# A hybrid decoder layer on one core: eight weight column groups in the opening instead of seven

## The chip, the core and the metric

The kernel runs on one core of one Trainium2 chip. Times are device microseconds of one whole execution. The kernel before took 734.72 us (median of three runs, 734.35 to 735.94). The profiled execution, from which all rows in this document come, took 734.0 us, of which 732.2 us are the profiled span.

The core's engines are called PE (TensorE), DVE (VectorE), ACT (ScalarE), POOL (GpSimd) and SP (SyncE, which only issues transfers here). Each runs its own list of instructions in order and waits on the others through semaphores. PE writes its results to eight banks of 128 x 512 float32 values (PSUM); ACT and DVE read them from there, and a bank can be given to new work only when it has been read.

## The reference

One post-norm decoder layer for a sequence of 512 tokens and 1024 channels. The input `x` is modulated by a condition vector `c`, projected once, and split into two attention branches:

```python
mod = c @ w_ada + b_ada
u = x * (1.0 + sc1) + sh1
proj = u @ w_in
q_a, k_a, v_a, f_a, q_b, k_b, v_b, g_a, g_b = jnp.split(proj, ...)
log_f = log_sigmoid(f_a + b_forget)                  # 8 forget logits a token
y_fox = softmax(q_a k_a^T / 8 + c_t - c_s) v_a       # 8 heads, c = cumsum(log_f)
y_sb  = stick_breaking(q_b k_b^T / 8) v_b            # 8 heads
merged = sigmoid(g_a) * (y_fox @ w_fox_proj) + sigmoid(g_b) * (y_sb @ w_sb_proj)
x = layer_norm(ALPHA * x + (1 + gt1) * (merged @ w_o))
...                                                  # gated MLP with a causal convolution, layer norm
```

`w_in` has 512 columns for each q, k, v of each branch, eight forget columns, and 1024 columns for each of the two gates `g_a`, `g_b`. A tile of 128 gate columns is called a gate tile here, so each branch has eight of them.

## The kernel before

Products are made in three passes to keep precision: every float32 operand is split into a high part and a low part (`h` and `l` of the weights, `uh` and `ul` of the activations), and each 128 x 128 by 128 x 512 product is the sum of high by high, low by high, high by low. ACT writes the high part (`hi_of`), DVE the low part (`lo_of`). In what follows "a product" is one such PE pass; a tile of 128 output columns over the eight 128-channel steps is 8 x 3 = 24 products.

**The opening** goes through the input channels in eight steps, j = 0 to 7. In each step it loads two rows of the adaLN weights (`wa`), one piece of input weights `w1[j]` of 128 rows by `W1C` columns, and 128 channels of the transposed input (`first_load`, all on SP's queue, whose order is the program's). DVE works out scale and shift of the step's channels (`first_acc`, `mod_col`), ACT and DVE split the weights and make `uh` and `ul` (`first_split`, `first_mod`), and PE multiplies for the column groups (`first_mm`). There are seven groups of 128 columns: q and k of the first stick-breaking head pair and gate tiles 0 to 4 of the stick-breaking branch. Each accumulates in its own bank, `grp[0]` to `grp[6]`. A step is thus 21 products. In step 0 banks 6 and 7 also hold the broadcast condition vector, until ACT has copied it.

The last eight of the `W1C` = 904 columns are the forget weights. ACT copies them out of each step's piece (`first_pad`) and in the last step `forget_mm` multiplies them, in plain float32, into bank 7, after groups 2, 0 and 1 and before groups 3 to 6. The forget bias `bfs` has a small load of its own behind step 6.

The opening's banks are read as the heads begin: gate 0 (`gate_after`, a sigmoid on ACT), q and k (`q_evac`, `k_evac`), the forget sums (`forget_evac`), and after the first scores gates 1 to 4. Their sigmoids wait in `sg` until the projected heads are multiplied by them.

**The heads** come next, eight of stick-breaking and eight of FoX, two to a pair. Each has three stages on PE: `stage_a` makes the scores (three banks; sigmoids or softmax follow on ACT, DVE and POOL), `stage_b` transposes the weights (three banks), `stage_c` multiplies by the values (one bank). In pass n of the loop the scores of head n + 2, the transposes of head n + 1 and the values of head n are made, so that ACT, DVE and POOL have a head's time for each.

Between the stages PE is filled from `stream`, a list of all other projections in a fixed order: q and k of the pairs to come, the value groups, the remaining gate tiles, later the branch projections. `fill(n)` draws products from it; `FILL` says how many after the scores, after the transposes and after the values. The generators hand products out three at a time (`yield 3`), and `fill` goes on while its count is above zero. `lim` keeps the list from running past a mark: up to the eighth head it ends behind q and k of pair 5 (`marks["y1"]`), and then `fill` returns early. `fill_to` draws until a tile that the next stage needs is done.

The weights of the list are loaded by SP in the list's order into five buffers and split ahead of their use (`weights`, `process`, `split_proc`). adaLN rows for later stages stand in the same list of loads (`add_ada`); DVE sums each when its turn comes. All engines but SP get the order of their work from a planner, which takes instructions by their place in the program and by its own estimate of when they are ready, and gives banks and buffers as they come free in that estimate.

Of the kernel before, what the change touches and what calls it, by code (L numbers as in the profile page):

```python
# [8 lines left out]
F32 = mybir.dt.float32  # L9
F32R = mybir.dt.float32r  # L10
BF16 = mybir.dt.bfloat16
AF = mybir.ActivationFunctionType
# [4 lines left out]
P = 128  # L17
T = 512
D = 1024
KT = D // P  # L20
# [5 lines left out]
NH = 8  # L26
ALPHA = 2.0 ** 0.25
EPS = 1e-5
NEG = -1.0e30
W1C = 904  # L30
NG = 5
PAIRS = [(1, p) for p in range(4)] + [(0, p) for p in range(4)]
TILES = [(c, p) for p in range(1, 8) for c in "qk"]
TILES += [("sb", j) for j in range(NG, KT)] + [("fox", j) for j in range(KT)]
NZ = 58
# [9 lines left out]
GTILES = (3, 5, 7, 8, 12, 16, 20, 24)  # L45
WARM = 5, 3, 1
CUT = 5
FILL = (15, 18, 18), (11, 11, 11)


@with_exitstack
def layer_kernel(ctx: ExitStack, tc: tile.TileContext, out, xT, x, c8, wa0, wa1, bcol, w1, wct, wv, bf,
                 wp, wo, lncol, lnrow, wup, cwb, wdp):
    nc = tc.nc
    ctx.enter_context(tc.manual_schedule(engines={nc.sync.engine}))
    V, S, G, PE = nc.vector, nc.scalar, nc.gpsimd, nc.tensor
# [12 lines left out]
    early = st0.enter_context(tc.tile_pool(name="early", bufs=1))  # L69
# [7 lines left out]
    def bank():  # L77
        return pp.tile([P, 512], F32, name=nm("ps"), tag="ps")
# [5 lines left out]
    def const(shape, dt, s):  # L84
        return cons.tile(shape, dt, name=s, tag=s)
# [4 lines left out]
    def hi_of(o, i, scale=1.0):  # L90
        S.activation(o, i, AF.Copy, scale=scale)
# [46 lines left out]
    with tc.issue_after(g.ins):  # L138
        G.memset(dg[:, 0:384], 0.0)
    G.tensor_copy(dg[:, 384:512], ident)  # L140
    bfs = const([NH, 1], F32, "bfs")
    modc = const([P, 4, KT], F32, "modc")
    modr = const([P, 6, KT, 2], F32, "modr")
    gcol, growt = [const([P, 32], F32, s) for s in ("gcol", "growt")]
# [78 lines left out]
    grp = [bank() for _ in range(8)]  # L223
    pend = {}

    fw = early.tile([P, KT, NH], F32, name="fw", tag="fw")
    us = []
    def heat(n):
        return [PE.matmul(grp[5], warm[:, 0:P], warm, start=True, stop=True) for _ in range(n)]

# [19 lines left out]
    def first_load(j):  # L250
        wa = [early.tile([P, D], F32, name=nm("wa"), tag="wa", bufs=5) for _ in range(2)]
        r = stg.tile([P, 1024], F32, name=nm("raw"), tag="raw", bufs=LOADS)
        xt = z(F32, "xt")
        if j == 0:
            for e in range(2):
                nc.sync.dma_start(wa[e], wa0[j, e])
            nc.sync.dma_start(r[:, 0:384], w1[j][:, 0:384])
            nc.sync.dma_start(x0, xT[j * P : (j + 1) * P, :])
            nc.sync.dma_start(r[:, 384:W1C], w1[j][:, 384:W1C])
        else:  # L260
            nc.sync.dma_start(wa[0], wa0[j, 0])
            if j == 1:
                nc.sync.dma_start(wa[1], wa0[j, 1])
            nc.sync.dma_start(r[:, 0:W1C], w1[j])
            if j > 1:
                nc.sync.dma_start(wa[1], wa0[j, 1])
            nc.sync.dma_start(xt, xT[j * P : (j + 1) * P, :])
            if j == 6:
                nc.sync.dma_start(bfs, bf)
        pend[j] = [wa, xt, r]  # L270

    def first_acc(j):
# [21 lines left out]
    def first_split(j):  # L294
# [3 lines left out]
        if j:  # L298
            hi_of(h[:, 0:W1C], r[:, 0:W1C])
        else:  # L300
# [3 lines left out]
    def first_pad(j):  # L304
        h, l, r = pend[j][2:]
        if j == 0:
            c = slice(384, W1C)
            state["after"] = lo_of(l[:, c], r[:, c], h[:, c])
        f = slice(W1C - NH, W1C)
        hi_of(fw[:, j, :], r[:, f])  # L310

    def first_mod(j):
        wa, xt = pend[j][0:2]
# [2 lines left out]
        if j:  # L316
            u = S.activation(a, xt, AF.Identity, bias=sh, scale=sc)
            h, l, r = pend[j][2:]
            with tc.issue_after(state["modc"].ins):
                state["after"] = lo_of(l[:, 0:W1C], r[:, 0:W1C], h[:, 0:W1C])  # L320
            with tc.issue_after(u.ins):
# [34 lines left out]
    def forget_mm(m):  # L356
        for k in range(KT):
            q = 32 * (k % 4)
            with tc.issue_after(m.ins):
                m = PE.matmul(grp[7][q : q + NH, :], fw[:, k, :], us[k], start=k < 4, stop=k > 3, tile_position=(0, q))  # L360
        return m

    def first_mm(j, gs):
        ops = [(g, n, m) for g in gs for n, m in enumerate(first_ops(j, g))]
        if j < KT - 1:
            rank = (0, 2, 4, 1, 3, 5)
            ops.sort(key=(lambda o: rank[o[1]] + 3 * (o[0] > 2) if o[0] < 5 else o[1]) if j == 0 else lambda o: o[1])
        for g, n, (w, u) in ops:
            m = PE.matmul(grp[g], w, u, start=j == 0 and n == 0, stop=j == KT - 1 and n == 2)  # L369
        return m  # L370
# [6 lines left out]
    for j in range(KT):  # L377
        if j + 2 < KT:
            first_load(j + 2)
        if j + 1 < KT:  # L380
            with tc.issue_after(state["u"].ins):
                first_split(j + 1)
            with tc.issue_after(state["after"].ins):
                first_acc(j + 1)
        if j < KT - 1:
            first_mm(j, range(5))
        if j + 1 < KT:
            first_mod(j + 1)
        if j < KT - 1:
            first_mm(j, range(5, 7))  # L390
        else:
            forget_mm(first_mm(j, (2, 0, 1)))
            first_mm(j, range(3, 7))

    st0.close()

# [257 lines left out]
        eng.dma_start(gt[i][:, c], grow[i][:, c].broadcast_to([P, (j1 - j0) * P]))  # L654
        yield 0

    sg, ma, wps = {}, {}, {}

    def gate_after(br, j):
        def f(ps):  # L660
            sg[(br, j)] = z(F32, "sg")
# [96 lines left out]
    def add_gate(br, j):  # L758
        add_proj(("sb" if br == 1 else "fox", j), gate_after(br, j))
        add_ada()  # L760

    gb = list(range(NG, KT))
    add_pair(1)
# [2 lines left out]
    add_pair(2)  # L766
    add_gate(1, gb.pop(0))
    add_pair(3)
    add_gate(1, gb.pop(0))
    add_pair(4)  # L770
    marks["vf"] = len(stream) + 2
    add_values(0, 0)
# [4 lines left out]
    for p, nb in (6, 3), (7, 5):  # L777
        add_pair(p)
        for _ in range(nb):
            j = bj.pop(0)  # L780
# [62 lines left out]
    forget_evac()  # L843
    fill(12)
    stage_a(1, 0)
    for j in range(1, NG):
        gate_after(1, j)(grp[2 + j])
    fill(18)
    stage_a(1, 1)
# [5 lines left out]
    for n, (b, h) in enumerate(heads):  # L855
        f1, f2, f3 = FILL[n // 8]
        if n + 2 < 16:
# [183 lines left out]
    for n in range(2 * FT):  # L1041
        wui.append(add_item(wup[n], split_proc))
        if n in GTILES:
            k = GTILES.index(n)
            wai[(10, 28)[k // 4]] = add_item(wa1[(28, 24)[k // 4] + k % 4], ada_proc((28, 24)[k // 4] + k % 4))
        if n in (15, 19):
            p = (15, 19).index(n)
# [8 lines left out]
        if n in (28, 31, 32, 35):  # L1056
            k = (28, 31, 32, 35).index(n)
# [117 lines left out]
    for n in range(2 * FT):  # L1175
        if n < NSPLIT:
            h, l = items[wui[n]][4]
            ps = bks[n]
            up_mm(ps, h, l, slice(256, 512))
        else:  # L1180
            ps = bank()
            h, l = weights(wui[n], min(LOADS - 1, wui[min(n + 2, 2 * FT - 1)] - wui[n]))
# [52 lines left out]
    r = x1  # L1235
# [136 lines left out]
def _pack(inputs):  # L1372
    import numpy as np

    a = {k: np.ascontiguousarray(v) for k, v in inputs.items()}
    c = np.ascontiguousarray
    w_in, w_ada = a["w_in"], a["w_ada"]
    r = {}
    r["xT"] = c(a["x"][0].T)
    r["x"] = a["x"][0]  # L1380
    r["c8"] = c(a["c"][0].reshape(KT, P))
    wt = c(w_ada.T).reshape(6, KT, P, D)
    wa0 = wt[0:2].transpose(1, 0, 2, 3).copy()
    wa0[0] = wa0[0].reshape(2, P, 2, D // 2).transpose(2, 1, 0, 3).reshape(2, P, D)
    r["wa0"] = c(wa0)
    r["wa1"] = c(wt[2:6].reshape(32, P, D))
    bm = a["b_ada"].reshape(6, KT, P)
    r["bcol"] = c(bm[[0, 1, 3, 4, 2, 5]].transpose(2, 0, 1))
    def col(kind, n):
        if kind in ("sb", "fox"):  # L1390
            return (4104 if kind == "sb" else 3080) + n * P
        br, p = PAIRS[n]
        return 1544 * br + 512 * "qkv".index(kind) + p * P

    first = [w_in[:, s : s + P] for s in [col("q", 0), col("k", 0)] + [col("sb", j) for j in range(NG)]]
    cols = np.concatenate(first + [w_in[:, 1536:1544]], axis=1)
    r["w1"] = c(cols.reshape(KT, P, W1C))
    wv = np.stack([w_in[:, 1024:1536], w_in[:, 2568:3080]])
    r["wv"] = c(wv.reshape(2, 4, 2, P, 512).transpose(0, 1, 3, 2, 4).reshape(2, 4, P, D))
    starts = [col(*t) for t in TILES]  # L1400
    r["wct"] = c(np.stack([w_in[:, s : s + P].reshape(KT, P, P).transpose(1, 0, 2).reshape(P, D) for s in starts]))
    r["bf"] = c(a["b_forget"].reshape(NH, 1))
    wpj = np.stack([a["w_fox_proj"], a["w_sb_proj"]]).reshape(2, 4, P, 4, 2, P)
    r["wp"] = c(wpj.transpose(0, 3, 2, 4, 1, 5).reshape(2, 4, P, D))
    r["wo"] = c(a["w_o"].reshape(KT, P, D))
    r["lncol"] = c(np.stack([a["ln1_g"].reshape(KT, P), a["ln1_b"].reshape(KT, P)]).transpose(2, 0, 1))
    r["lnrow"] = c(np.stack([a["ln1_g"], a["ln1_b"], a["ln2_g"], a["ln2_b"]]))
    wu = a["w_up"].reshape(KT, P, 2, FT, P)
    r["wup"] = c(wu.transpose(3, 2, 1, 0, 4).reshape(2 * FT, P, D))
    cwb = np.concatenate([a["conv_w"], a["conv_b"][None]], axis=0).reshape(4, 2, FT, P)  # L1410
    r["cwb"] = c(cwb.transpose(3, 2, 1, 0).reshape(P, 2 * FT, 4))
    wd = a["w_down"].reshape(FP, 2, P, 2, 512)
    b11, b12, b21, b22 = [wd[:, m, :, n] for m in range(2) for n in range(2)]
    r["wdp"] = c(np.concatenate([b11, b12, b22, b21], axis=2))
    return r


_NAMES = ["xT", "x", "c8", "wa0", "wa1", "bcol", "w1", "wct", "wv", "bf", "wp", "wo", "lncol", "lnrow",
          "wup", "cwb", "wdp"]


# [17 lines left out]
```

## Time and profile before

| | |
|---|---|
| median of three runs | 734.72 us (734.35 to 735.94) |
| profiled execution, and its span | 734.0 us, 732.2 us |
| PE busy | 722.6 us, 99% of the span |
| DVE, ACT, POOL busy | 601.1, 391.7, 88.1 us |
| opening: first to last product before the forget sums | 7.93 to 44.1 us |
| first scores of a head | 51.7 us |
| scores of the ninth, tenth and eleventh head | 175.2, 190.5, 201.0 us |
| granted PE clock | full in every fortieth of the span |

"Busy" is time in which an engine had an instruction under way; a matmul's end is modelled, so the start of one product to the start of the next says more than its duration. Rows of single instructions give start, duration, engine, line, operation, output and inputs, count, and in brackets the idle time before it and what ended that. On the page tile names stand without their numbers: `wh`, `wl` are split weights, `ps` is a bank, `pt` the head's weights, `ph`, `pl` their transposed parts, `m` and `s` the k and q of a head.

### The profile page before, as it was taken

What the parts mean: (1) busy time and instruction counts of PE and PEld (TensorE: products, weight loads), DVE (VectorE), ACT (ScalarE), POOL (GpSimd) and SP (SyncE); (2) the same over time, 40 slices, a digit from 0 to 9 for tenths busy, and PEclk for the clock granted to TensorE, in tenths of its full rate; (3) what the DMA queues carried; (4) which work ended last, traced back from release to release, by engine and by line L of the source; (5) the groups of instructions that cost most, each with busy time, mean ns of one, the idle gap of its engine ahead of it and who ended that gap; (6) DMA issues with size and microseconds to landing.
All of it is one profiled execution on the core that took longest, in us unless ns stands there. A gap on an engine that the chain in (4) does not pass through costs nothing.

```text
span 732.2 us, 9844 instructions
## 1 busy us (share of the span) xinstructions
PE 722.6 (99%) x3444; PEld 602.3 (82%) x3444; DVE 601.1 (82%) x1041; ACT 391.7 (53%) x684; POOL 88.1 (12%) x142
## 2 busy tenths in 40 slices
PE   8999999999999999999999999999999999999996
PEld 5878888888888888888889888888888888888885
DVE  7978799778898886873697999978887787679996
ACT  5576466686885754442056553444453544347550
POOL 1045224352010000000000001000011010000010
PEclk9999999999999999999999999999999999999999
DMA  9953535423332241632075688577699777646733
GB/s 354 404 208 126 175 116 196 149 88 115 118 116 100 75 170 60 228 124 86 1 259 143 205 250 250 162 249 227 200 349 252 210 239 209 203 161 227 223 89 92
DMA packets 45490, 131.96 MB, mean 180 GB/s; under 512 B 6168, under 2 KB 7200, under 8 KB 45440
## 3 DMA queue, kind: packets, MB, share of 16 engines
q1 hardware_dynamic: 38176, 112.61, 44.6%
q0 software_dynamic: 4224, 10.30, 7.0%
q10 hardware_dynamic: 3040, 8.42, 3.1%
q8 instruction: 27, 0.44, 0.2%
q14 instruction: 23, 0.19, 0.1%
HBM read 118.39 MB, written 12.85 MB: 179 GB/s over the span
## 4 chain that ended last, share of the span: by engine, by line
PE 97%; DMA 1%; DVE 1%; ACT 0%; issue 0%; DVEq 0%
PE ps L152 19%; PE ps L154 19%; PE ps L153 19%; PE ps L1152 5%; PE ps L1153 5%; PE ps L1154 5%; PE ps L369 5%; PE ps L613 3%; PE ps L595 2%; PE ps L521 2%; PE ps L523 2%; PE ps L522 2%; PE ps L944 2%; PE ps L945 2%; PE ps L943 2%; PE ps L547 1%
## 5 line engine op out<-in xcount | busy, mean ns | idle before, releaser
L217 ACT ACTIVATE wh<-raw 128x1024 fp32r<-128x1024 f32 (+1 forms) x105 | 109.1, 1041 | 105.0 <-PE ps L153 47.2
L94 DVE TENSOR_TENSOR wl<-raw,wh 128x1024 fp32r<-128x1024 f32 (+2 forms) x114 | 137.2, 1204 | 30.6 <-ACT wh L217 29.5
L152 PE MATMUL ps<-u2h,wh 128*128 128x512 f32 (+1 forms) x376 | 141.3, 376 | 0.0
L153 PE MATMUL ps<-u2l,wh 128*128 128x512 f32 (+1 forms) x376 | 141.2, 375 | 0.0
L154 PE MATMUL ps<-u2h,wl 128*128 128x512 f32 (+1 forms) x376 | 141.2, 375 | 0.0
L153 PEld LDWEIGHTS ps<-u2l,wh 128*128 128x128 f32 x376 | 70.8, 188 | 12.8
L154 PEld LDWEIGHTS ps<-u2h,wl 128*128 128x128 f32 x376 | 70.8, 188 | 12.8
L152 PEld LDWEIGHTS ps<-u2h,wh 128*128 128x128 f32 x376 | 70.8, 188 | 12.7
L152 PE MATMUL ps<-uh,wh 128*128 128x512 f32 x200 | 79.5, 397 | 0.0
L154 PE MATMUL ps<-uh,wl 128*128 128x512 f32 x200 | 78.1, 391 | 0.0
L153 PE MATMUL ps<-ul,wh 128*128 128x512 f32 x200 | 77.9, 390 | 0.0
L1205 ACT ACTIVATE cv<-ps,cw 128x512 f32<-128x512 f32 x44 | 34.0, 774 | 48.1 <-PE ps L154 40.9
L1206 DVE SCALAR_TENSOR_TENSOR cv<-ps,cw,cv 128x511 f32<-128x511 f32 x44 | 32.8, 746 | 23.0 <-ACT cv L1205 23.0
L154 PEld LDWEIGHTS ps<-uh,wl 128*128 128x128 f32 x200 | 37.5, 188 | 8.3
L153 PEld LDWEIGHTS ps<-ul,wh 128*128 128x128 f32 x200 | 37.6, 188 | 7.4
L152 PEld LDWEIGHTS ps<-uh,wh 128*128 128x128 f32 x200 | 37.5, 188 | 7.4
L240 DVE SCALAR_TENSOR_TENSOR raw<-raw,cbc 128x1024 f32<-128x1024 f32 x32 | 39.6, 1240 | 0.0
L575 POOL TENSOR_TENSOR pt<-pt,om 128x127 f32<-128x127 f32 (+3 forms) x32 | 38.6, 1217 | 1.4 <-DVE om L574 1.3
L181 POOL DMA_DIRECT2D raw<-in_wdp x10 | 8.9, 886 | 244.6 <-DMA raw<-in_wdp 228.1
L1207 DVE SCALAR_TENSOR_TENSOR cv<-ps,cw,cv 128x510 f32<-128x510 f32 x44 | 32.8, 744 | 0.4
L574 DVE TENSOR_TENSOR_SCAN om<-om,dg 128x127 f32<-128x127 f32 (+3 forms) x32 | 28.9, 962 | 3.8 <-ACT om L569 3.8
L1218 ACT ACTIVATE cv<-cv 128x512 f32<-128x512 f32 x21 | 13.3, 631 | 32.0 <-DVE cv L1207 32.0
(246 smaller groups left out, 1551.8 us busy)
## 6 DMA issues: line engine op xcount, KB each, us to landing
raw<-in_wup SPq DMA_DIRECT2D x44, 512.0 KB, 5.0
raw<-in_wa SPq DMA_DIRECT2D x32, 512.0 KB, 3.6
raw<-in_wct SPq DMA_DIRECT2D x25, 512.0 KB, 4.6
raw<-in_wdp SPq DMA_DIRECT2D x20, 512.0 KB, 5.2
wa<-in_wa SPq DMA_DIRECT2D x16, 512.0 KB, 8.7
raw<-in_wdp SPq DMA_DIRECT2D x22, 256.0 KB, 4.7
raw<-t SPq DMA_DIRECT2D x22, 256.0 KB, 4.7
raw<-in_wdp POOLq DMA_DIRECT2D x10, 512.0 KB, 7.7
```

The costliest lines, as they stand in the source:

```text
L94: state["read"] = V.tensor_tensor(o, i, fl(hi), ALU.subtract)
L152: PE.matmul(ps, wh, ah, start=first, stop=False)
L153: PE.matmul(ps, wh, al, start=False, stop=False)
L154: return PE.matmul(ps, wl, ah, start=False, stop=last)
L217: state["hi"] = S.activation(h[:, 0:cols], r[:, 0:cols], AF.Copy)
L240: state["read"] = V.scalar_tensor_tensor(wt[:, c], wt[:, c], 1.0, cbc[:, c] if by is None else by, ALU.mult, ALU.mult, accum_out=o)
L369: m = PE.matmul(grp[g], w, u, start=j == 0 and n == 0, stop=j == KT - 1 and n == 2)
L575: G.tensor_tensor(pt[b][:, s : e - 1], pt[b][:, s : e - 1], om[:, s + 1 : e], ALU.mult)
L1152: PE.matmul(ps, ah, bh, start=first, stop=False, skip_group_check=onto)
L1153: PE.matmul(ps, ah, bl, start=False, stop=False, skip_group_check=onto)
L1154: return PE.matmul(ps, al, bh, start=False, stop=last, skip_group_check=onto)
L1205: tap = S.activation(t, ps, AF.Identity, bias=cw[:, n, 3:4], scale=cw[:, n, 2:3])
```

## The change

The opening takes eight groups of 128 columns: gate tile 5 of the stick-breaking branch joins it, in bank 7 (`W1C` = 1024, `NG` = 6). Its tile leaves the list `stream`; the adaLN row that stood behind it stays. The forget weights leave `w1` and come in one load of 128 x 65 float32 values, which also carries the bias, at the place of the bias's load; the eight copies on ACT go. In the last step the order of PE becomes group 7, 0, 1, then 2 and 3, the forget products, then 4 to 6; the sigmoid of group 7 is issued within the opening, since the forget products use its bank again. `FILL` of the stick-breaking heads becomes 15, 17, 16.

```diff
-W1C = 904
-NG = 5
+W1C = 1024
+NG = 6
...
-FILL = (15, 18, 18), (11, 11, 11)
+FILL = (15, 17, 16), (11, 11, 11)
...
-    bfs = const([NH, 1], F32, "bfs")
+    fwt = const([P, KT * NH + 1], F32, "fwt")
+    fw = fwt[:, 0 : KT * NH].rearrange("p (k h) -> p k h", h=NH)
+    bfs = fwt[0:NH, KT * NH : KT * NH + 1]
...
-    fw = early.tile([P, KT, NH], F32, name="fw", tag="fw")
-    us = []
+    us, sg, ma = [], {}, {}
...
-                nc.sync.dma_start(bfs, bf)
+                nc.sync.dma_start(fwt, fwb)
...
-        f = slice(W1C - NH, W1C)
-        hi_of(fw[:, j, :], r[:, f])
...
         if j < KT - 1:
-            first_mm(j, range(5, 7))
+            first_mm(j, range(5, 8))
         else:
-            forget_mm(first_mm(j, (2, 0, 1)))
-            first_mm(j, range(3, 7))
+            first_mm(j, (7, 0, 1))
+            sg[(1, NG - 1)] = z(F32, "sg")
+            S.activation(sg[(1, NG - 1)], grp[7], AF.Sigmoid)
+            forget_mm(first_mm(j, (2, 3)))
+            first_mm(j, range(4, 7))
...
     add_gate(1, gb.pop(0))
     add_pair(3)
-    add_gate(1, gb.pop(0))
+    add_ada()
     add_pair(4)
...
-    for j in range(1, NG):
+    for j in range(1, NG - 1):
         gate_after(1, j)(grp[2 + j])
```

The packing on the host follows: `w1` has the eight groups without the forget columns, and `fwb` holds the forget weights as 128 x 64 values with the bias in a 65th column.

More of the change, by code (lines that the diff above doesn't have):

```diff
@@ L47, with layer_kernel @@
 CUT = 5
-FILL = (15, 18, 18), (11, 11, 11)
+FILL = (15, 17, 16), (11, 11, 11)
 @with_exitstack
-def layer_kernel(ctx: ExitStack, tc: tile.TileContext, out, xT, x, c8, wa0, wa1, bcol, w1, wct, wv, bf,
+def layer_kernel(ctx: ExitStack, tc: tile.TileContext, out, xT, x, c8, wa0, wa1, bcol, w1, wct, wv, fwb,
                  wp, wo, lncol, lnrow, wup, cwb, wdp):
@@ L655, in gate_rows @@
         yield 0
-    sg, ma, wps = {}, {}, {}
     def gate_after(br, j):
@@ L1395, in _pack @@
     first = [w_in[:, s : s + P] for s in [col("q", 0), col("k", 0)] + [col("sb", j) for j in range(NG)]]
-    cols = np.concatenate(first + [w_in[:, 1536:1544]], axis=1)
+    cols = np.concatenate(first, axis=1)
+    fwb = np.zeros((P, KT * NH + 1), np.float32)
+    fwb[:, 0 : KT * NH] = w_in[:, 1536:1544].reshape(KT, P, NH).transpose(1, 0, 2).reshape(P, KT * NH)
+    fwb[0:NH, KT * NH] = a["b_forget"]
+    r["fwb"] = fwb
     r["w1"] = c(cols.reshape(KT, P, W1C))
@@ L1401, in _pack @@
     r["wct"] = c(np.stack([w_in[:, s : s + P].reshape(KT, P, P).transpose(1, 0, 2).reshape(P, D) for s in starts]))
-    r["bf"] = c(a["b_forget"].reshape(NH, 1))
     wpj = np.stack([a["w_fox_proj"], a["w_sb_proj"]]).reshape(2, 4, P, 4, 2, P)
@@ L1415, in _pack @@
     return r
-_NAMES = ["xT", "x", "c8", "wa0", "wa1", "bcol", "w1", "wct", "wv", "bf", "wp", "wo", "lncol", "lnrow",
+_NAMES = ["xT", "x", "c8", "wa0", "wa1", "bcol", "w1", "wct", "wv", "fwb", "wp", "wo", "lncol", "lnrow",
           "wup", "cwb", "wdp"]
```

## The prediction

> **What bounds the kernel now.** I read the page's first lines, then the stretches of the span, then who TensorE (PE) waits for, and last the order of single instructions at the two places that the change touches.
>
> ```profile
> span 732.2 us, 9844 instructions
> PE 722.6 (99%) x3444; PEld 602.3 (82%) x3444; DVE 601.1 (82%) x1041; ACT 391.7 (53%) x684; POOL 88.1 (12%) x142
> PE 97%; DMA 1%; DVE 1%; ACT 0%; issue 0%; DVEq 0%
> ```
>
> PE is busy for 99% of the span and is 97% of the chain that ended last. Work that only moves from one stretch of PE to another is worth nothing unless one of the two has gaps. The stretches say where (start:end and length, then busy time and instructions of PE, weight load, VectorE, ScalarE, GpSimd; granted clock, DMA share, GB/s):
>
> ```profile
> 18.20:42.10 23.90, 23.90 (x106) 19.79 (x106) 21.66 (x41) 14.16 (x22) 3.86 (x8) 1.00 1.03 406
> 51.70:175.20 123.50, 123.50 (x612) 104.42 (x611) 103.05 (x139) 81.44 (x148) 50.80 (x75) 1.00 0.41 141
> 175.20:201.00 25.80, 25.80 (x134) 22.03 (x133) 21.38 (x52) 21.96 (x43) 2.10 (x4) 1.00 0.35 125
> 284.00:732.20 448.20, 440.97 (x2053) 369.00 (x2051) 363.74 (x618) 203.52 (x332) 24.72 (x36) 1.00 0.61 192
> ```
>
> From 18.2 us on the opening leaves PE no idle time, and neither do the heads from 51.7 to 201; VectorE is at 83% there. Who PE waits for, over the whole span, in total us, times, longest:
>
> ```profile
> PE ps L229 <- DVE warm L107: 1.2, 1, 1.2
> PE ps L229 <- DVE wa L240: 0.7, 2, 0.4
> PE ps L369 <- DVE uh L331: 0.3, 1, 0.3
> PE ps L369 <- ACT uh L317: 0.2, 1, 0.2
> ```
>
> The heads (scores L546, transposes L595, values L613, filling L152) are not in this list at all. All that PE can gain lies in the first steps of the opening:
>
> ```profile
> 12.34 0.61 PE L369 MATMUL ps<-ul,wh 128*128 128x512 f32 x2
> 13.20 1.43 PE L369 MATMUL ps<-uh,wh 128*128 128x512 f32 x5 [0.25 <-ACT uh L317]
> 18.20 1.39 PE L369 MATMUL ps<-uh,wh 128*128 128x512 f32 x5
> 23.06 1.30 PE L369 MATMUL ps<-uh,wh 128*128 128x512 f32 x5
> 27.82 1.30 PE L369 MATMUL ps<-uh,wh 128*128 128x512 f32 x5
> ```
>
> Steps j = 1, 2, 3 begin at 13.20, 18.20, 23.06, and j = 4 at 27.82. A step has 21 products. The last interval, 4.76 us, is the bare one: 4.76 / 21 = 0.2267 us a product. The excess of the others is waiting: step 0 should hand over at 12.34 + 2 x 0.2267 = 12.79 (0.41 lost), step 1 loses 0.24, step 2 0.10: 0.75 us in all.
>
> **The change, part by part.**
>
> *24 products join the opening.* Three in each of eight steps, 24 x 0.2267 = +5.44 us of PE. Their operands come later in the first steps:
>
> ```profile
> 11.48 0.96 ACT L91 ACTIVATE wh<-raw 128x904 fp32r<-128x904 f32 x1 [1.86 <-DMA raw<-in_w]
> 14.83 0.68 DVE L94 TENSOR_TENSOR ul<-xt,uh 128x512 fp32r<-128x512 f32 x1
> 49.45 1.21 DVE L94 TENSOR_TENSOR wl<-raw,wh 128x1024 fp32r<-128x1024 f32 x1
> ```
>
> For step 1 the SP queue must bring two widened weight pieces, 2 x 120 columns x 128 x 4 B = 123 KB, 0.30 us at 406 GB/s. ScalarE's split, which waits for them, then begins at 11.78 and takes 0.96 x 1024/904 = 1.09 at most, and `uh`, behind it on ScalarE, moves by 0.30 + 0.13 = 0.4, and PE's step 1 with it: 13.6. Step 0 now keeps PE until 12.79 + 0.68 = 13.47: 0.14 lost instead of 0.41. `ul` of step 1 moves by the 0.4 of its `wh` and the 0.11 by which VectorE's split grows (1.21 by the row of 1024 columns, 1.10 in proportion for 904), so it ends at 14.83 + 0.68 + 0.5 = 16.0, where PE, ten products after 13.6, would be ready at 15.9: 0.2 lost with the hand-over. From step 2 on PE needs 24 x 0.2267 = 5.44 us a step, while the loads need 1.84 MB / 406 GB/s = 4.5 and VectorE's share of 18.2 to 42.1 grows from 21.66 by five times 0.11 in a stretch that is now longer: PE falls behind its inputs and waits for none. So 0.34 us are lost where 0.75 were: -0.41. Bounds: -0.75 (no gap left) to +0.5 (both delays in full).
>
> *The forget weights' load.* It removes eight small copies:
>
> ```profile
> L91 ACT ACTIVATE fw<-raw x8: 191/192/204, 9.4 to 42.6; 128x8 f32<-128x8 f32 x8
> 43.97 0.60 ACT L662 ACTIVATE sg<-ps 128x512 f32<-128x512 f32 x1 [0.26 <-PE ps L369]
> 43.46 0.93 PE L369 MATMUL ps<-ul,wh 128*128 128x512 f32 x3
> 46.15 0.50 PE L369 MATMUL ps<-uh,wh 128*128 128x512 f32 x1
> 50.69 0.74 DVE L419 SCALAR_TENSOR_TENSOR fq<-ps,bfs,fq 8x512 f32<-8x512 f32 x1
> 51.72 0.22 PE L546 MATMUL ps<-m,s 128*128 128x128 f32 x1
> ```
>
> They are off PE's path: 0. The new load, 33 KB in place of the bias alone, is one issue on SP behind `xt` of step 6, 0.08 us at 406 GB/s, issued near 27 us and first read after 46: 0, and it would take some 15 us of delay to show. The forget products sit between 43.46 + 3 x 0.2267 = 44.14 and 46.15, 2.0 us; they now share bank 7 with the new gate, whose sigmoid must have read it. Queued behind that wait on PE are the nine products of groups 4 to 6. Twelve products (groups 0 to 3, 2.7 us) cover one sigmoid (0.60 in the row): 0; without them it would cost that 0.6.
>
> Rule and row differ on small pieces. The load's rows are 65 x 4 = 260 B a partition.
>
> ```profile
> cw<-in_cwb SPq DMA_DIRECT2D x1, 88.0 KB, 3.7
> lnc<-in_lncol SPq DMA_DIRECT2D x1, 8.0 KB, 4.0
> ```
>
> `lnc` (64 B a partition) lands in 4.0 us, `cw` (704 B) in 3.7: no sign of a penalty, and 4.0 us fit the cover. The Trainium skill, DMA: Bandwidth & Descriptors, section Specifications, wants at least 512 B a piece for line rate, below which it says the engines read, modify and write. By that rule the load and its neighbours on the queue would be slower; with a whole us of it on a queue that is ahead of PE the sum would still be the same.
>
> *What is late next.* From the end of group 1 to the first scores (51.72) PE used to run 2.0 us of forget products and 24 others; now 2.0 and 27, but ScalarE gets the new sigmoid, and the old group 2 is read after groups 0 and 1. The forget products' end to the scores shrinks from 24 products (46.15 to 51.72) to 21, so `fq`, at 51.43 the last to free a bank, has 0.68 us less. Bounds: 0 (its ScalarE copies wait less behind others now) to +1.0 (two sigmoids of 0.6 ahead of it, less the 0.3 to spare). I take 0, since groups 0 and 1 are no later relative to the scores.
>
> *24 products leave the heads, but not 3 a head.* Every generator of the stream hands out three products at a time, and the filling stops once the count has reached zero or below. 17 asked gives 6 x 3 = 18, 16 gives 18. The heads still draw 15 + 18 + 18 = 51, and the stream, one tile shorter, runs dry earlier. Counting through the list, nothing changes in the filling's amounts until after the values of the seventh head (of stick-breaking pair 3): there 18 drawn become 6, and after the scores of the tenth 12 become 0. After the values of the eighth head the list stands where it stood. These are the places:
>
> ```profile
> 185.14 0.56 PE L613 MATMUL ps<-ph,vv 128*128 128x512 f32 x2
> 186.36 0.45 PE L152 MATMUL ps<-uh,wh 128*128 128x512 f32 x1
> 190.52 0.22 PE L546 MATMUL ps<-m,s 128*128 128x128 f32 x1
> 194.55 1.25 PE L595 MATMUL ps<-ident,pt 128*128 128x128 f32 x10
> 195.56 0.65 PE L613 MATMUL ps<-ph,vv 128*128 128x512 f32 x2
> 196.86 0.44 PE L152 MATMUL ps<-uh,wh 128*128 128x512 f32 x1
> 201.00 0.22 PE L546 MATMUL ps<-m,s 128*128 128x128 f32 x1
> ```
>
> 18 products took 190.52 - 186.36 = 4.16 us, 0.231 each; 24 x 0.231 = -5.54 at most, -5.44 by the opening's pitch; I take -5.44 and keep 0.1. On the clock of before, less the common shift, the scores of head ten come at 186.36 + 6 x 0.231 = 187.7, the transposes of head nine at 189.0, the values of head eight at 190.0, the next tile (q of pair 6) at 191.3, the next scores at 195.4. What they need:
>
> ```profile
> 181.91 1.27 DVE L564 TENSOR_SCALAR pt<-pt,sm 128x128 f32<-128x128 f32 x4
> 184.17 0.55 DVE L94 TENSOR_TENSOR pl<-ps,ph 128x384 fp32r<-128x384 f32 x1
> 183.87 1.28 ACT L662 ACT_TABLE_LOAD   x1
> 194.60 0.71 ACT L559 ACTIVATE pt<-pt,sm 128x512 f32<-128x512 f32 x1
> 195.43 2.42 ACT L91 ACTIVATE m<-ps 64x512 fp32r<-64x512 f32 x4
> 197.88 1.41 DVE L94 TENSOR_TENSOR m<-ps,m 64x512 fp32r<-64x512 f32 x2 [0.96 <-ACT m L91]
> ```
>
> The softmax that the transposes read is done at 183.2 (5.8 us to spare), the low parts for the values at 184.7 (5.3). The scores at 195.4 need k of pair 5, whose last product begins before 187.7; its four copies take 2.42 and the differences 1.41: some 191.9 if they go straight away, 3.5 to spare. So 0, with a top bound in the first rival. Elsewhere the tile order shifts by one tile against the heads; ScalarE and VectorE lose a split each. One buffer is held longer for the early gate: 0.
>
> Sum: +5.44 - 0.41 - 5.44 = -0.4 us. The profiled execution took 734.0 (1.8 around its span), the median is 734.72, 0.7 above it; moved alike, 733.6 and 734.3.
>
> **The rivals.**
>
> *Slower: the uncovered stretch stalls.* After head ten's scores PE has no filling. In the trace, k's copies start (195.43) only when the last exponential is over (195.31). If they stay behind it, the exponentials end 195.31 - 190.52 = 4.8 us after the scores begin, at 192.5; copies and differences follow to 192.5 + 3.9 = 196.4. Scores wait 1.0 us; and where the next tile is given k's bank (eight banks: three for scores, three for transposes, one for values, one for k), it waits from 191.3 to 196.4: 5.1. Time 735.3 to 739.4. For it: that order in the trace, eight banks full. Against: k's products now end before the scores begin, so its copies are ready first, and a scores bank comes free early. It decides once the copies begin later than 195.4 - 3.9 = 191.5.
>
> The table load at 183.87 and its like go if the gate's sigmoid now precedes the softmax: 2 x 1.28 = 2.6 us of ScalarE here. ScalarE: Activation LUTs (the Trainium skill), What ACT_TABLE_LOAD costs, counts 2.66 us for each switch with its drain, so 5.3; the trace starts the sigmoid 1.29 us after the load began. Either speaks a little against this rival.
>
> *A bank is late at the first scores:* +1.0 on the sum, 735.3.
>
> *Opening gains all:* no gaps at steps 1 and 2, -0.75, less the 0.1: 733.9.
>
> *Faster by more:* a gain must come where PE still idles, 448.20 - 440.97 = 7.2 us after 284, if the shifted order reaches there. A fifth of it with the opening's 0.41 gives 734.72 - 1.4 - 0.4 = 732.9. No edit touches that stretch.
>
> *The change as written,* 48 a head: the same products, only spread; 734.3 too.
>
> **How the numbers follow.** 734.3 with 0.58 (own range 733.6 to 735.6); slower rival 0.18; late bank 0.08; all gaps 0.08; faster by more 0.08. A measurement tells 0.2%, 1.5 us, from no change: 733.25 to 736.2. Slower is the rival where it costs more than 1.9, 0.14, with 0.04 of other tails: 0.18. Faster: 0.08 and 0.02 of tails. Same: 0.72. The range 733.0 to 737.0 leaves out the dearer half of the slower rival and most of the faster.
>
> **What would show it.** Step intervals of 5.44 us from step 2 on, and no PE wait later. 51 products around heads one to six, 6 between values seven and scores ten, then transposes straight away. A PE gap at the tile after the values of head eight would be the slower rival; one at the first scores the late bank. Intervals of 48 products a head, or a stall inside heads one to six, would make my reading wrong.

## The result, and the profile after

The change made the kernel slower: 737.62 us (median of six runs, 737.14 to 738.57) against 734.54 us for the kernel before on the same chip (six runs, 734.21 to 735.94). The ratio is 1.0041, with a 95% interval of 1.0028 to 1.0054, so 3.1 us were lost where 0.4 were to be gained. 737.62 lies outside the predicted range of 733.0 to 737.0. The profiled execution took 737.61 us.

The page of the kernel after, its span and the busy time of its engines, and the chain that ended last by engine:

```profile
span 735.8 us, 9825 instructions
PE 723.3 (98%) x3444; PEld 602.1 (82%) x3444; DVE 600.8 (82%) x1040; ACT 387.0 (53%) x673; POOL 88.3 (12%) x142
PE 94%; ACT 3%; DVE 1%; DMA 1%; issue 0%; SPq 0%; DVEq 0%; ACTq 0%
```

PE was 97% of the chain before and is 94% now; ACT grew from 0% to 3%. Something other than PE now sets the end for some 3% of 736 us, and the time itself rose by less, because PE works through part of it. Where that lies, the stretches say. Cut at the first scores and at the scores of the sixth and the eighth head (start:end and length, then PE, weight load, DVE, ACT, POOL, clock, DMA), first before:

```profile
51.72:129.28 77.56, 77.56 (x381) 65.46 (x380) 67.53 (x92) 47.27 (x88) 30.12 (x43) 1.00 0.46 160
129.28:159.89 30.61, 30.61 (x155) 25.98 (x154) 23.48 (x30) 24.36 (x41) 12.04 (x16) 1.00 0.33 110
```

and after, between the same instructions of the heads:

```profile
57.09:134.65 77.56, 77.56 (x382) 65.46 (x380) 64.44 (x89) 45.35 (x86) 30.52 (x43) 1.00 0.38 131
134.65:168.30 33.65, 31.66 (x155) 25.77 (x154) 27.57 (x36) 26.94 (x43) 14.95 (x23) 1.00 0.48 167
```

The first stretch has kept its length to a hundredth. The second has the same 155 products and takes 33.65 us instead of 30.61: 3.04 us, as much as the whole loss. The list of what PE waited for from 60 to 300 us, empty before, now has two entries (total, times, longest):

```profile
PE ps L154 <- ACT wh L219: 1.4, 1, 1.4
PE ps L525 <- DVE wl L94: 0.5, 1, 0.5
```

Both are split weights that come late: first those of k of pair 4 (the first FoX pair), then those of a value tile. The chain of waits of after between 127 and 150 us tells what they were late for (start, length, what):

```profile
130.54 0.68 DVE m L94
...
131.42 0.43 issue
131.86 1.23 DVE raw L242 x2
...
133.10 3.25 DMA raw<-in_wct
...
136.37 1.06 ACT wh L219
```

The load of k's weights (`raw<-in_wct`) begins at 133.10, directly behind a sum over an adaLN row on DVE (`raw`, L242), takes 3.25 us, and only then ACT can split it. Before, the same load went out at 112.41, which on the clock of after, 5.37 us later in these heads, is 117.78. SP's queue, before and then after, around this tile:

```profile
111.99 0.33 SPq L174 DMA_DIRECT2D raw<-in_wa  x1
112.41 0.38 SPq L174 DMA_DIRECT2D raw<-in_wct  x1
```

```profile
115.07 0.33 SPq L176 DMA_DIRECT2D raw<-in_wct  x1
115.49 0.38 SPq L176 DMA_DIRECT2D raw<-in_wa  x1
133.10 0.33 SPq L176 DMA_DIRECT2D raw<-in_wct  x1
```

Between 115.87 and 133.10 SP issues no load of the list. The code says why. A load is held until the item four places ahead of it in the list has been read (`paced`, `depth`). The change takes the gate tile out of "k of pair 3, row, gate tile, row, q of pair 4, row, k of pair 4" but leaves its row, so the list now reads "k, row, row, q, row, k". Four places ahead of the last k now stands the row behind the first k; before, it was the gate tile, split early. And an adaLN row is not read when its turn comes: `process` holds it until the next weight tile is split, which for both rows is now q of pair 4, whose own load went out only at 115.07. Its split ends on DVE at 120.82; the two sums are given places on DVE behind the evacuation of k of pair 3 (`m`), at 131.86 and 133.00.

### The profile page after: what moved, and what is told of

Its sections match the earlier page's. It is cut to its first block, busy times and chain, and to the rows that moved or that the text cites. A ratio compares the mean times of both kernels' runs of the same rounds, so it can differ in the third digit from the quotient of the medians.

```text
span 735.8 us, 9825 instructions
## 1 busy us (share of the span) xinstructions
PE 723.3 (98%) x3444; PEld 602.1 (82%) x3444; DVE 600.8 (82%) x1040; ACT 387.0 (53%) x673; POOL 88.3 (12%) x142
## 4 chain that ended last, share of the span: by engine, by line
PE 94%; ACT 3%; DVE 1%; DMA 1%; issue 0%; SPq 0%; DVEq 0%; ACTq 0%
PE ps L154 18%; PE ps L156 18%; PE ps L155 18%; PE ps L369 6%; PE ps L1155 5%; PE ps L1153 5%; PE ps L1154 5%; PE ps L616 2%; PE ps L598 2%; PE ps L946 2%; PE ps L944 2%; PE ps L945 2%; PE ps L524 2%; PE ps L526 2%; PE ps L525 2%; PE ps L550 1%
## 5 line engine op out<-in xcount | busy, mean ns | idle before, releaser
L219 ACT ACTIVATE wh<-raw 128x1024 fp32r<-128x1024 f32 x104 | 108.0, 1040 | 105.8 <-PE ps L155 40.2
L154 PE MATMUL ps<-uh,wh 128*128 128x512 f32 x192 | 76.5, 398 | 1.4 <-ACT wh L219 1.4
L156 PE MATMUL ps<-uh,wl 128*128 128x512 f32 x192 | 75.2, 392 | 0.0
L155 PE MATMUL ps<-ul,wh 128*128 128x512 f32 x192 | 74.8, 390 | 0.0
L156 PEld LDWEIGHTS ps<-uh,wl 128*128 128x128 f32 x192 | 36.0, 188 | 8.1 <-DVE wl L94 0.2
L155 PEld LDWEIGHTS ps<-ul,wh 128*128 128x128 f32 x192 | 36.1, 188 | 7.1
L242 DVE SCALAR_TENSOR_TENSOR raw<-raw,cbc 128x1024 f32<-128x1024 f32 x32 | 39.4, 1235 | 0.0
```

Source lines behind the costliest of these rows:

```text
L154: PE.matmul(ps, wh, ah, start=first, stop=False)
L155: PE.matmul(ps, wh, al, start=False, stop=False)
L156: return PE.matmul(ps, wl, ah, start=False, stop=last)
L219: state["hi"] = S.activation(h[:, 0:cols], r[:, 0:cols], AF.Copy)
L242: state["read"] = V.scalar_tensor_tensor(wt[:, c], wt[:, c], 1.0, cbc[:, c] if by is None else by, ALU.mult, ALU.mult, accum_out=o)
```

## The experiments

The theory at this point, *pacing*: the two rows side by side hold k's load back. Its rival, *shift*: one tile fewer in the list moves every split, bank and chain against the heads, and the stall would come whatever stands there. Times are compared with runs of the kernel before on the same chip, 734.36 to 734.63 us.

**The rows together, in the kernel before.** The opening and the number of tiles stay; only the gate tile goes ahead of pair 3 and leaves its row, so q and k of pair 3 come one tile later.

```diff
+    add_proj(("sb", gb[0]), gate_after(1, gb.pop(0)))
     add_pair(3)
-    add_gate(1, gb.pop(0))
+    add_ada()
     add_pair(4)
```

> The kernel before, with seven groups, and only this: the second gate tile of the list goes ahead of pair 3 and its adaLN row stays behind pair 3, so that two rows stand together ahead of pair 4, while q and k of pair 4 keep their places against the heads. Pacing theory: the load of k of pair 4 waits for a held row, PE waits for that tile's split between 129 and 140 us, and the time rises by 1.5 to 3.5 us to 736 to 738. Shift rival: nothing that it blames is there, 734.5 (734.0 to 735.0).

741.51 us, ratio 1.0098 (1.0085 to 1.0112): the stall comes with the two rows side by side and nothing else of the change, and larger than expected. Waits, and the stretches around it:

```profile
PE ps L152 <- ACT wh L217: 4.7, 1, 4.7
```

```profile
136.88:141.95 5.07, 0.39 (x3) 0.00 (x1) 4.82 (x10) 3.21 (x5) 0.00 (x0) 0.86 0.61 175
142.00:146.40 4.40, 4.40 (x11) 3.30 (x12) 2.30 (x3) 1.02 (x1) 0.00 (x0) 0.50 0.62 213
```

It is the same tile and the same line of code. Here its load goes out only at 137.56, where before it went out at 112.41: the two sums stand at 136.31 and 137.45, again behind the evacuation of k of pair 3 (135.00), which comes one tile later in this list. The stall is paid twice: 5.07 us pass from one product's start to the next, and then the granted clock is still 0.50 over the 4.4 us of the second row, which has 11 products where 19 would fit at 0.2267. The gaps of after, 1.79 us at most, left the clock at 1.00.

**One row moved, and rows not held, in the kernel after.**

```diff
     add_pair(3)
-    add_ada()
     add_pair(4)
 ...
     add_values(0, 0)
+    add_ada()
     add_gate(1, gb.pop(0))
```

> The changed kernel, with one edit: the extra adaLN row that took the gate's place behind pair 3 stands behind the values of the FoX branch instead, so that no two rows stand together ahead of pair 4. The tiles keep their new places against the heads. Pacing theory (the load of k of pair 4 stands four places behind a row that is held until the next split, and waits for that row's sum): the load goes out before 125 us, PE has no wait in the stretch of 134 to 163, and the time falls by the 3.0 us lost there, to 734.6 (734.0 to 735.2). Shift rival (tiles come 24 products earlier against the heads, where ScalarE and VectorE are fuller, and splits are late whatever the loads do): at least half of the 3.0 stays, 736 to 737.6.

```diff
-        f.late = n < 24
+        f.late = n < 24 and n not in (8, 9)
```

> The changed kernel with the two rows together, but these two are not held until the next split: their sums are issued as their turn comes, behind the split before them. Pacing theory: the sums come before the copies of k of pair 3 are waited for, the load of k of pair 4 goes out some 8 us earlier, before 126 us, and 2 to 3 of the 3.0 us come back: 734.6 to 735.6. Shift rival: 736 to 737.6.

735.74 us (ratio 1.0019, 1.0010 to 1.0028) and 736.09 us (1.0024, 1.0013 to 1.0035). In both the wait at k is gone: with the rows read at once (the second of the two kernels) their sums stand at 118.31 and 119.46 and the load goes out at 119.56, not 133.10. So the hold is what delayed the load. But both are slower than the theory alone had it, 734.0 to 735.2 and 734.6 to 735.6 us. A wait is left, the same in both; in the first of them:

```profile
155.08 0.60 PE L598 MATMUL ps<-ident,pt 128*128 128x128 f32 x4
156.51 1.10 PE L598 MATMUL ps<-ident,pt 128*128 128x128 f32 x6 [0.83 <-ACT pt L573]
```

The transposes of the sixth head stop after four, because the next bank is still held by the seventh head's scores, which ACT has not read. What ACT did instead, in the same kernel:

```profile
146.95 1.28 ACT L429 ACT_TABLE_LOAD   x1
...
149.51 1.28 ACT L430 ACT_TABLE_LOAD   x1
...
154.08 1.28 ACT L572 ACT_TABLE_LOAD   x1
155.37 0.60 ACT L572 ACTIVATE om<-ps 128x512 f32<-128x512 f32 x1
```

This is the forget gate's chain (`fq`: Abs, Exp, Ln), with a change of function table ahead of Exp and of Ln, and a third ahead of the sigmoids that read the scores' banks. In the kernel before, the seventh head's sigmoids came first:

```profile
147.25 0.60 ACT L569 ACTIVATE om<-ps 128x512 f32<-128x512 f32 x1
...
150.34 1.28 ACT L426 ACT_TABLE_LOAD   x1
```

The chain is tied in the code to the split of the third value tile, and every tile after the missing one comes one tile earlier against the heads. The second theory, *forget chain*: this alone costs about 1.3 us. In both kernels the eighth head's scores follow the seventh's after 16.59 us, where before took 15.31; the other intervals of the first eight heads are those of before.

**The gate tile left in the middle.** Opening and everything else as after; gate tile 7 of the branch takes the place of the missing one, so that the list is the old one up to k of pair 4 and the values, and a row alone stands behind the values.

```diff
     add_pair(3)
-    add_ada()
+    add_gate(1, gb.pop(0))
     add_pair(4)
 ...
-    add_gate(1, gb.pop(0))
+    add_ada()
```

> The changed kernel, but the gate tile of the list keeps its place between pairs 3 and 4, and the one behind the FoX values goes, its row staying. Until the values the list is that of the kernel before, tile and row in turn. Both theories: no wait at k of pair 4, 734.6 (734.0 to 735.2). If it is slower than 736, neither theory holds and the stall comes from the opening's side.

734.74 us, ratio 1.0004 (0.9995 to 1.0013): no wait of PE in the heads. Both causes are gone, since both come from the place in the list that was emptied. The wide opening as such shows neither a cost nor a gain beyond that interval, 0.4 us faster to 1.0 slower.

**The chain by itself, in the kernel before.** One edit, the chain tied to the split of the second value tile.

```diff
-            late = br == 0 and j == 2
+            late = br == 0 and j == 1
 ...
-    marks["vf"] = len(stream) + 2
+    marks["vf"] = len(stream) + 1
```

> The kernel before, with one edit: the forget gate's chain tied to the split of the second value tile instead of the third, one tile earlier against the heads, as the change does it. Nothing else moves, the opening and the list stay. Theory of the forget chain: ScalarE loads a table again ahead of the sigmoids of the sixth or seventh head's scores, the transposes that follow wait, and the time rises by 0.5 to 1.5 us, to 734.9 to 735.9 us. Rival, that the chain's place is nothing by itself and only the shifted list costs: 734.2 to 734.6 us.

736.31 us, ratio 1.0023 (1.0015 to 1.0032). From the seventh head's scores to the fifth head's values, in the kernel before and then in this one:

```profile
144.60:154.50 9.90, 9.90 (x52) 8.40 (x51) 7.29 (x11) 9.79 (x19) 5.70 (x8) 1.00 0.18 55
```

```profile
144.37:156.32 11.95, 10.54 (x52) 8.31 (x51) 10.51 (x14) 10.92 (x20) 5.23 (x8) 1.00 0.13 45
```

```profile
150.38 0.63 PE L595 MATMUL ps<-ident,pt 128*128 128x128 f32 x4 [1.15 <-DVE m L94]
151.27 1.10 PE L595 MATMUL ps<-ident,pt 128*128 128x128 f32 x6 [0.26 <-ACT pt L570]
```

The same 52 products take 2.05 us longer, and the transposes wait at the same place. A table load stands ahead of the sigmoids again (at 148.83). The cost is above the 0.5 to 1.5 expected. Here the chain also stands ahead of k's copies on ACT, which begin at 146.43 (144.84 before): the first wait, 1.15 us, is put down to the differences on DVE that follow those copies, and only the second to the sigmoids.

**The chain one tile later.** Once on top of the moved row, once alone on the kernel after.

```diff
-            late = br == 0 and j == 2
+            late = br == 0 and j == 3
 ...
-    marks["vf"] = len(stream) + 2
+    marks["vf"] = len(stream) + 3
```

> The kernel after, with the second adaLN row issued behind the first block of values (as in e1_row_after_values, 735.74 us) and the forget gate's chain (Abs, Exp, Ln with its two table loads on ScalarE) tied to the split of the fourth value tile instead of the third, one tile later. Theory of the forget chain: at 155.42 in the trace of after a third table load stands ahead of the sigmoids of the seventh head's scores, because the chain runs before them; one tile later the sigmoids go first, the wait of 0.8 at the transposes behind them is gone with the 1.3 us around it, and the time is 734.2 to 734.9 us. Rival, that the tile order itself (one tile earlier against the heads, its banks and its loads) makes the rest of the loss: the wait stays and the time is 735.5 to 736.0 us.

> The kernel after with one edit: the forget gate's chain tied to the fourth value tile's split, the two rows left where the change puts them. Two separate causes, pacing and the chain: the stall of 2.5 us around k of the fifth pair (1.40 + 0.53 of waits) stays, the one of 0.5 us at the transposes behind the seventh head's scores goes, and the time is 736.9 to 737.3 us. If the chain were the whole of the loss the time would be 734.5 us; if it were none of it, 737.6 us.

On top of the moved row: 734.68 us, ratio 1.0004 (0.9995 to 1.0012), and no wait of PE in the heads. The sigmoids stand ahead of the chain's Exp again:

```profile
152.88 0.57 ACT L572 ACTIVATE om<-ps 128x512 f32<-128x512 f32 x1
...
155.43 1.28 ACT L429 ACT_TABLE_LOAD   x1
```

The profiled execution took 736.17; what it lost stands in the opening (first scores at 59.02, 57.09 in after), and from there to the eighth head's scores it takes 108.17 us, as before does. So the loss of after is taken away, within the interval, by two edits that touch neither the opening nor the number of tiles, and the rival *shift* is left with 0.9 us at most. Alone on the kernel after, the later chain brings nothing: 738.12 us, ratio 1.0045 (1.0033 to 1.0057), 0.8 above what was expected. From the sixth to the eighth head's scores its profile still loses 2.90 us of the 3.04. Exp and two table loads stand ahead of the sigmoids as in after, and the sigmoids begin at 157.50: counted from the first scores and against the run on top of the moved row, the seventh head's scores come 2.67 us later, but Exp's table load only 0.75.

```profile
154.27 1.28 ACT L429 ACT_TABLE_LOAD   x1
...
156.21 1.28 ACT L572 ACT_TABLE_LOAD   x1
```

This run therefore doesn't separate the two costs in after. The chain of waits of after does, in part: it goes through Ln's table load at 152.00 and the sigmoids' at 155.42 to the transposes of the sixth head. Of the 3.04 us, 2.53 had been lost by the seventh head's scores (17.83 us behind the sixth's, where before took 15.30) and 0.51 came behind them (the ten transposes of the sixth head take 1.52 us to the next product, 1.01 before); so the delay at k seems to cover part of what the chain costs by itself (read from the numbers, not tested), and taking away the delay at k alone gave 1.9 us back and left 1.4.

**A true 48 a head.** On the kernel with the gate in the middle, amounts that threes divide.

```diff
-FILL = (15, 17, 16), (11, 11, 11)
+FILL = (15, 15, 18), (11, 11, 11)
```

> The kernel e2_gate_in_middle (734.74 us) with the filling of heads one to eight at 15, 15 and 18 products, which threes divide, so that each of these heads gets 48 and not 51 as with 15, 17 and 16. Theory that the intervals between heads are set by the number of products alone while loads and softmax are early: the heads one to six end 0.69 us earlier each, what is left over fills heads seven to ten, no new wait, and the time stays at 734.4 to 735.0 us. Rival, that three products fewer a head expose a wait (the transposes behind the scores, or k of a pair against the marks): 735.2 to 737 us.

735.23 us, ratio 1.0009 (1.0000 to 1.0018). In the heads there is one wait of 0.2 us (for the values' low parts on DVE, at the first head), and from the first scores to the last values 224.97 us instead of 224.44: no gain, and some half a microsecond more, as between the two medians (735.23 and 734.74). The change's own amounts, 17 and 16, never took effect, since threes make 18 of both.

**What the wide opening's loads cost.** In after the first product starts at 8.15 us, in before at 7.93; the kernels with the wide opening lie between 8.15 and 9.27, those with the old one between 7.73 and 7.97, with one profile each. Theory, *width*: the first step's last piece, 320 KB instead of 260, shares the transfer engines with the first 384 columns and `x`. Tried first by the order, on the kernel with the gate in the middle:

```diff
-            nc.sync.dma_start(r[:, 0:384], w1[j][:, 0:384])
             nc.sync.dma_start(x0, xT[j * P : (j + 1) * P, :])
+            nc.sync.dma_start(r[:, 0:384], w1[j][:, 0:384])
```

> The kernel e2_gate_in_middle (after, with the seventh gate tile where it was and a row behind the values; 734.74 us), with the first step's two loads exchanged: x ahead of the first 384 weight columns. Theory that the wider last piece of the first weight tile (640 columns for 520) holds x back, and with it the first product (8.15 us in after, 7.93 in before): the first product comes back to 7.9 to 8.0 and the time falls by 0.2 to 0.3 us, to 734.4 to 734.6 us. Rival, that the start is bounded by the weights' piece, which now lands later: first product at 8.2 or later and 734.7 to 735.1 us.

735.17 us, ratio 1.0006 (0.9997 to 1.0015), first product at 8.66: the wait went from `x` to the weights. Then by cutting the piece, on the two kernels without stalls:

```diff
-            nc.sync.dma_start(r[:, 384:W1C], w1[j][:, 384:W1C])
+            nc.sync.dma_start(r[:, 384:896], w1[j][:, 384:896])
 ...
                 nc.sync.dma_start(wa[1], wa0[j, 1])
+                nc.sync.dma_start(pend[0][2][:, 896:W1C], w1[0][:, 896:W1C])
```

> The kernel e8_row_moved_forget_later (734.68 us) with the first weight tile's last piece cut: columns 384 to 896 at its place, the 128 columns of the seventh gate tile behind the next step's two adaLN loads. Theory that the wider piece (320 KB for 260) and what follows it hold back x and the first 384 columns (landing 4.9 to 5.9 us after their issue in the kernels with the wide opening, 4.5 to 4.7 in those with the old one): landing 4.7 or less, first product at 8.1 or earlier, time 733.9 to 734.5 us. Rival, that the start depends on the next step's adaLN loads and not on this piece: landing and first product as in the other wide openings (8.15 to 9.0), 734.5 to 735.0 us.

> The kernel e2_gate_in_middle (734.74 us) with the same cut of the first weight tile's last piece. Theory that the wider piece holds the start back: first product at 8.1 or earlier instead of 8.31, time 734.2 to 734.6 us. Rival, that it doesn't: 734.6 to 735.0 us.

736.77 us (ratio 1.0038, 1.0026 to 1.0050) and 736.90 us (1.0036, 1.0024 to 1.0048): both 2 us worse. First products at 8.15 and 8.47, but the split of the 640 columns now waits for the piece put back, in the first of them:

```profile
10.84 0.74 ACT L337 ACTIVATE wh<-raw 128x640 fp32r<-128x640 f32 x1 [2.58 <-DMA raw<-in_w]
```

The edit moved the wait and made it larger, so it says nothing of the theory. Last, the width alone: the kernel before, loading 1024 columns a step and using 904 (the host packs 120 more).

```diff
-            nc.sync.dma_start(r[:, 384:W1C], w1[j][:, 384:W1C])
+            nc.sync.dma_start(r[:, 384:1024], w1[j][:, 384:1024])
 ...
-            nc.sync.dma_start(r[:, 0:W1C], w1[j])
+            nc.sync.dma_start(r, w1[j])
```

> The kernel before, whose opening loads 1024 weight columns a step instead of 904, the last 120 of them used by nothing; splits, products and the list of tiles are those of before. Theory that the wider loads by themselves hold back the start: the first 384 columns and x land later than the 4.6 and 5.0 us of before, the first product starts at 8.1 to 8.6 instead of 7.93, and the time rises by 0.2 to 0.6 us, to 734.6 to 735.1 us. Rival, that the load's width is nothing and the later start of the wide openings comes from their wider splits and their products: first product at 8.0 or earlier, landing as in before, 734.2 to 734.6 us.

735.78 us, ratio 1.0020 (1.0011 to 1.0029): more than expected. How long the first transfers took from issue to landing (KB each, us), in before and then in this kernel:

```profile
x<-in_xT SPq DMA_DIRECT2D x1, 256.0 KB, 5.0
raw<-in_w SPq DMA_DIRECT2D x1, 192.0 KB, 4.6
```

```profile
x<-in_xT SPq DMA_DIRECT2D x1, 256.0 KB, 5.7
raw<-in_w SPq DMA_DIRECT2D x1, 192.0 KB, 5.5
```

`x` and the first columns, issued ahead of the widened piece and no larger than before, land 0.7 and 0.9 us later, and the first product starts at 8.66. The same holds across all profiles: `x` lands after 4.8 to 5.0 us in the three kernels with the old loads, and after 5.2 to 6.4 in the seven with the new ones in the same order. The width costs 1.35 us in the medians where steps have 21 products. In the profile the first scores come 1.76 us later (53.48 for 51.72): 0.73 at the start, 0.33 more at step 1 (14.26 for 13.20) and 0.70 in later steps. In after, with 24 products a step, the gaps behind the start shrink in spite of it. The seven profiles of the same wide opening start up to 1.1 us apart, so how much the start costs after (0.22 in its profile) on the average of executions stays open.

No version measured beats the kernel before. The best two, 734.68 and 734.74 us, are level with it.

## Why the prediction was wrong

*24 products join the opening.* The size was right: the steps of after start 5.44 us apart from step 2 on, as forecast.

```profile
8.15 0.93 PE L369 MATMUL ps<-uh,wh 128*128 128x512 f32 x3 [0.46 <-DVE uh L331]
13.85 1.43 PE L369 MATMUL ps<-uh,wh 128*128 128x512 f32 x5
19.65 1.29 PE L369 MATMUL ps<-uh,wh 128*128 128x512 f32 x5
25.09 1.29 PE L369 MATMUL ps<-uh,wh 128*128 128x512 f32 x5
57.09 0.22 PE L549 MATMUL ps<-m,s 128*128 128x128 f32 x1
```

From the first product to the first scores are 48.94 us, where before had 43.79: 5.15 more, so 0.29 of gaps were gained and not 0.41 (step 1 lost 0.36, not 0.2: 19.65 - 13.85 - 5.44). The start, 0.22 later, the prediction did not have: it followed the wider loads into step 1 and not into step 0. The first scores came 5.37 later instead of 5.03, inside the bounds given.

*The forget weights' load* and *what is late next*, both at 0: right. The first scores follow the forget products' end by three products less than before (57.09 - 52.17 = 4.92 after 5.57), with no wait; the late bank did not come.

*24 products leave the heads, but not 3 a head.* The amounts were right, and so was the place where they go. The rounding to threes keeps 51 products around the heads, and the list runs dry where it was said. The slower rival's stretch, in after:

```profile
193.53 0.56 PE L616 MATMUL ps<-ph,vv 128*128 128x512 f32 x2
194.75 0.45 PE L154 MATMUL ps<-uh,wh 128*128 128x512 f32 x1
196.19 0.22 PE L549 MATMUL ps<-m,s 128*128 128x128 f32 x1
197.46 1.25 PE L598 MATMUL ps<-ident,pt 128*128 128x128 f32 x10
199.77 0.44 PE L154 MATMUL ps<-uh,wh 128*128 128x512 f32 x1
203.91 0.22 PE L549 MATMUL ps<-m,s 128*128 128x128 f32 x1
```

Six products between values and scores, transposes right behind, the next scores at 203.91 with no wait: the 5.5 us came as computed, and the rival's mechanism (k of pair 5 behind the softmax) did not occur: k's copies begin at 197.25 on ACT, ahead of the exponentials at 199.69. The prediction gave "slower" to the wrong place.

The step that failed is the end of that part: "Elsewhere the tile order shifts by one tile against the heads; ScalarE and VectorE lose a split each. One buffer is held longer for the early gate: 0." That shift, put at 0, cost 3.04 us between the scores of the sixth and the eighth head, where the prediction itself said a stall would prove its reading wrong. It counted products, splits and buffers, and left out two things in the list that are not products: the loads, which are paced by what is read four places ahead, and the forget chain, which is tied to a tile. The trace of before would have shown the first: the load at 111.99 goes out 0.03 us behind the end of a row's sum (110.74 + 1.22 in the trace of before), with that of k of pair 4 next, so loads there follow reads and not free transfer time.

One rival rested on a misreading. The 7.2 us without PE behind 284 us, from which *faster by more* took its gain, are not gaps that a shifted order could reach: from 284 to 720 us PE is busy without a break, and the last product of before starts at 724.70, 7.5 us ahead of the end of the span.

The account, from offsets of after against before: +5.37 at the first scores, +3.04 in the heads one to six, -5.50 in heads seven to ten, and +0.20 behind the heads, which makes 3.11 at the last product (724.70 to 727.81). The medians differ by 3.08.

## What to carry to other kernels

A list that PE draws work from is also the order of loads, of the buffers' release and of small chains tied to its items. Taking an item out changes who stands so many places ahead of whom, so go through the loads one by one, and ask of each what it is held for. Side work that is not multiplied (here the adaLN rows and the forget gate) belongs in that walk with the place it gets on its engine, because a late sum and a table load at the wrong moment cost here as much as 13 products (3.04 us at 0.2267 each). And where PE is full on both sides, moving products brings only the gaps of the place they go to, here 0.3 us.

## What the runs showed of the hardware

In the kernel before with the rows together, PE's last product ahead of the gap ended at 137.27. Its granted clock was 0.99 from 140.0 to 140.5 us and 0.50 from 140.5 on, so it fell after some 3.2 us of idling; PE worked again from 141.95, and the clock was 0.50 up to 147.3 and 1.00 from 147.45, so it came back after some 5.4 us of work. The gap of 1.79 us in after left it at 1.00. So a gap of 5 us cost 7.2 (741.51 against 734.36). The Trainium skill, TensorE: Matmul & The Clock Gate, section What's actually happening, says the clock halves after an idle window of about 3.4 us and is full again after at least one busy window of the same length. The 3.2 us agree with the first; the way back took longer here than one such window.

A change of ACT's function table took 1.28 us in every row, and the instruction behind it began 1.29 us after the load's start (154.08 to 155.37). The Trainium skill, ScalarE: Activation LUTs, section What ACT_TABLE_LOAD costs, counts 1.28 us for the load and 1.38 more for a drain; the drain doesn't show in these rows. The order matters more than the size: the three loads are 3.8 us of ACT. They cost PE 1.28 us with the row moved and 2.02 with the chain moved in the kernel before (from the seventh to the eighth head's scores), where they stood ahead of the sigmoids that free its banks (in the second of k's copies too), and nothing with the row moved and the chain later, where the sigmoids came first.

With 60 KB more in the loads behind them, two unchanged transfers landed 0.7 and 0.9 us later (one profile of each kernel). At the some 400 GB/s that the engines move there, 60 KB are 0.15 us, by estimate; the weights of the next step, 512 KB for 452, were on their way by then too. What makes the delay so much larger was not settled.
